# The mixer's output projection as seven half-size products, with the weight sums made in DRAM

## The chip, the cores and the metric

The kernel runs on one core of a Trainium2 chip. The metric is the device time of one execution in microseconds. Three runs of the kernel before took 1121.22, 1121.75 and 1121.85 us. Five engines with queues of their own work side by side: PE (matmul), DVE (elementwise, two inputs), ACT (elementwise, one input, activation functions), POOL, and SP, which here only issues DMAs. PE and DVE and ACT meet through SBUF and through the eight banks of PSUM, each of 128 x 512 floats.

## The reference, cut to what matters

A decoder block on x of shape 1024 tokens x 1024 channels in float32. A mixer makes `merged`, its output projection `mix` goes through a norm into the residual, and an MLP with squared ReLU follows:

```python
merged = (g_pool * jnp.einsum('bsc,cd->bsd', y_pool, w_branch_pool[l])
          + g_attn * jnp.einsum('bsc,cd->bsd', y_attn, w_branch_attn[l]))
mix = jnp.einsum('bsd,de->bse', merged, w_out[l])
x = x + _rmsnorm(mix, g_mix_post[l])
h2 = _rmsnorm(x, g_mlp_pre[l])
ff = jnp.einsum('bsf,fd->bsd', jnp.square(jax.nn.relu(jnp.einsum('bsd,df->bsf', h2, w_up[l]))), w_down[l])
x = x + _rmsnorm(ff, g_mlp_post[l])
```

The change is about the line `mix = ...`, a 1024 x 1024 x 1024 product, and about what it hands to the up projection (`w_up`, 1024 x 4096).

## The kernel before, in words

**Precision.** Each float32 operand is split into a high part (a cast to the reduced type F32R on ACT) and a low part (source minus high, on DVE): `split`, L99 to L104. Every product is made of three passes, high x high, high x low and low x high (`PASSES`, L32). So a 128 x 128 x 512 block costs three matmuls, and every operand costs one ACT and one DVE instruction.

**Stages in order.** Projections for q, k, v and the pooling; attention; the gates; the two branches; the output projection; the up projection; the down projection. The gates, the up and the down projection already run as seven half-size products in place of eight (Winograd's form of Strassen's scheme). The class `Pairs` (L444) does it for gates and up: two output row blocks (a pair p) take two half-size products M1 and M2 (`m1`, `m2`) and then five more (`rest`, L505), whose moving operands are sums of the halves of the activations: B11, B21, B22 as they are and T1 to T4 as sums (`OPERAND`, L442), and whose weights are sums made on DVE in SBUF (`operand`, L458).

**Branches (L897 to L955).** For each of eight channel blocks m a weight block is loaded and split, 24 matmuls of 512 columns run into two PSUM banks, and DVE multiplies with the gate (`branch`, L902). The attention branch makes eight results `za[m]`; then the pool branch makes eight more. `merge` (L928) adds the two halves of the tokens, on POOL for m < 6 and on DVE for m = 6 and 7, and splits the sum: 16 splits of 512 columns.

**Output projection (L963 to L1018 and L1123 to L1138).** Eight blocks of `w_o` are loaded through three staging slots (`stage`, pool `st`) and split (`load_wo`, L940). For each of eight token blocks n, `out_mm` (L986) issues 8 x 3 x 2 = 48 matmuls of 512 columns into two banks. `out_post` (L999) squares the two banks for the norm on ACT, scales them on DVE from PSUM, adds x, stores x1 to DRAM, and scales by the gate's factor into `hs[n]`. Within token block 5 the transposes of the first four token blocks stand (`build_first`, L1044, eight calls, four 128 x 128 transposes each). In `n == 5` up pairs 0 to 2 are prepared.

**Start of the up projection (L1163 to L1201).** M1 and M2 of six pairs (NF0 = 6) run early, as they need only B11 and B21. In their shade `build_second` (L1054) transposes the second four token blocks and makes T2, T1, T3, B22, T4. Then `rest` closes pair after pair.

**What sets the order.** The attention and the first part of the gates are written out by hand. Everything from the `rest` of the gates on is ordered by a planner, which places each instruction when its own estimates say that it can run, in program order among those that are ready; an engine then works through its queue in that order. Buffers are counted: four PSUM banks under the name `mm` and four under `at`, three staging slots `st`, 17 slots `g`, six `wh`, six `ga`, four `y`.

Of the kernel before, what the change touches and what calls it, by code (L numbers as in the profile page):

```python
# [14 lines left out]
P = 128  # L15
# [35 lines left out]
def block_kernel(ctx: ExitStack, tc, xt, x, consts, vecs, sinks, b_qkv, g_post, g_mlp_post,  # L51
                 w_qkv, w_u, w_g, w_pool, w_bp, w_ba, w_o, w_up, w_dn, x1_dram, spill, y_dram, wbp_dram, f_dram, out):
# [391 lines left out]
    class Pairs:  # L444
# [7 lines left out]

        def load(self, f, t=None):
            t = stage([NK, P]) if t is None else t
            nc.sync.dma_start(t, self.src[f])
            self.raw[f] = t

        def operand(self, p, i):  # L458

            r0, r1_ = self.raw[2 * p], self.raw.get(2 * p + 1)  # L460
            if i in (5, 6, 3):
                if p not in self.sums:
                    self.sums[p] = ga_.tile([P, 2, 4, P], F32, tag="ga", name=nm("ws"))
# [371 lines left out]

    def later_builds():
# [60 lines left out]
    def gate_load(m):  # L897
        t = g32([S])
        nc.sync.dma_start(t, z_dram[m])
        return t  # L900

    def branch(w, rhs, z):  # L902
# [3 lines left out]
        for th in range(2):  # L906
            sl = slice(th * 512, (th + 1) * 512)
            dve.tensor_tensor(z[:, sl], z[:, sl], bs[th], ALU.mult)
        return z
# [11 lines left out]
    ysp, za = {}, []  # L921
    for m in range(8):
        za.append(branch(w_ba[m], lambda k, hl, th: asp[th][k // 2][hl][:, k % 2, :], gate_load(8 + m)))
        if m in (2, 3, 5, 6):
            pool_part({2: 1, 3: 0, 5: 2, 6: 3}[m])
    mg = []

    def merge(m, zp):  # L928
        mt = []
        for th in range(2):  # L930
            sl = slice(th * 512, (th + 1) * 512)
            (pool if m < 6 else dve).tensor_tensor(zp[:, sl], zp[:, sl], za[m][:, sl], ALU.add)
            t = ar([2, 512]) if th == 1 and 1 <= m <= 6 else gr([2, 512])
            split(t[:, 0, :], t[:, 1, :], zp[:, sl])
            mt.append(t)
        mg.append(mt)

    wos = []

    def load_wo(k, tile_):  # L940
        s_ = stage([D])
        nc.sync.dma_start(s_, w_o[k])
        hi, lo = tile_("wohi"), tile_("wolo")
        split(hi, lo, s_)
        wos.append((hi, lo))

    def wo_early(name):
        return yy.tile([P, D], F32R, tag="y", name=nm(name))
# [14 lines left out]
    for k in range(2, NK):  # L963
        if k == 3:
            merge(7, zp)
            gpost_b = bcast(g_post, D)
        load_wo(k, lambda name: wo.tile([P, D], F32R, tag="wo", name=nm(name)))
# [16 lines left out]
    obs = {}  # L984

    def out_mm(n, ks):  # L986
        th, i = n // 4, n % 4
        if n not in obs:
            tag = "at" if n in (0,) else "mm"
            obs[n] = bank(tag), bank(tag)  # L990
        for k in ks:
            for hl in range(2):
                l = mg[k][th][:, hl, i * P:(i + 1) * P]
                for whl in range(2 - hl):
                    for dj in range(2):
                        pe.matmul(obs[n][dj], l, wos[k][whl][:, dj * 512:(dj + 1) * 512],  # L996
                                  start=k == 0 and hl == 0 and whl == 0, stop=k == NK - 1 and hl == 1)

    def out_post(n):  # L999

        bs = obs.pop(n)
        xs = stage([D])
        nc.sync.dma_start(xs, x[n])
        t = (bcp.tile([P, D], F32, tag="bc", name=nm("x1")) if n == 4 else
             xq.tile([P, D], F32, tag="x1", name=nm("x1")))
        r = mean_sq(bs, halves(t))
        for dj in range(2):
            sl = slice(dj * 512, (dj + 1) * 512)
            dve.scalar_tensor_tensor(t[:, sl], bs[dj], r, gpost_b[:, sl], ALU.mult, ALU.mult)
# [3 lines left out]
        hs[n] = t  # L1013
# [24 lines left out]
    def tr_block(th, k):  # L1038
        b = bank("at", [4, P])
# [4 lines left out]
    def build_first(kt, h):  # L1044
        if h == 0:
            raw[kt] = g32([2, 512])
        k = 4 * h + kt
        b = tr_block(0, k)
# [5 lines left out]
    def build_second(kt):  # L1054
        b12, b22 = tr_block(1, kt), tr_block(1, 4 + kt)
        if kt % 2:
            tmp = stage([2, 512])
        else:
            tmp = ga_.tile([P, 2, 512], F32, tag="ga", name=nm("tt"))
# [5 lines left out]
        dve.scalar_tensor_tensor(t3, b22, gain(4 + kt), t3, ALU.mult, ALU.subtract)  # L1065
        dve.tensor_tensor(r21, r21, t2, ALU.subtract)
        for name, src in (("T2", t2), ("T1", r11), ("T3", t3), ("B22", b22), ("T4", r21)):
            if name == "B22":
                t = ar([2, 512])
            else:  # L1070
                t = (yy.tile([P, 2, 512], F32R, tag="y", name=nm(name)) if kt == 0 else
                     fp.tile([P, 2, 512], F32R, tag="T", name=nm(name)))
            if name == "B22":
                split_gain(t, src, 4 + kt)
            else:
                split(t[:, 0, :], t[:, 1, :], src)
            X[name][kt] = t

# [38 lines left out]
    def up_big(shape):  # L1117
        return xq.tile([P] + shape, F32R, tag="x1", name=nm("wx"))

    up = Pairs(w_up, up_big, lambda: g32([S]), up_close_first, up_close0, up_close1)  # L1120
    X = up.X

    for ks in (range(NK - 1), range(NK - 1, NK)):  # L1123
        out_mm(0, ks)
        out_mm(1, ks)
    out_post(0)
    out_post(1)
    for n in range(2, NT):
        if n == 5:
            for k in range(NK):  # L1130
                out_mm(n, (k,))
                build_first(k // 2, k % 2)
        else:
            out_mm(n, range(NK))
        out_post(n)
        if n == 5:
            for p in range(3):
                up.prepare(p)  # L1138
# [5 lines left out]
    gfin_b = bcast(g_mlp_post, D)  # L1144
    NP = NF // 2
    NF0 = 6
# [24 lines left out]
    for p in range(3):  # L1171
        up.m1(p, bank("mm"))
    build_second(0)
    up.m2(0)
    up.m1(3, bank("mm"))
    build_second(1)
    up.m2(1)
    up.m1(4, bank("mm"))
    up.prepare(5)
    up.operand(0, 6)  # L1180
    b6, b7 = bank("at"), bank("at")
    build_second(2)
    up.m2(2)
    for i in (7, 5, 4, 3):
        up.operand(0, i)
    up.m2(4)
    up.m1(5, bank("mm"))
    first_kt(0)
    build_second(3)
    up.m2(3)  # L1190
    first_kt(1)
    up.m2(5)
    first_kt(2)
    first_kt(3)
# [5 lines left out]
    up.rest(0, ga_.tile([P, S], F32, tag="ga", name="f1_first"), b6, b7, bank("at"), done=(6, 7),  # L1200
# [28 lines left out]
    flush()  # L1229
    fpool.__exit__(None, None, None)  # L1230
# [233 lines left out]
```

## Time and profile before

| what | value |
|---|---|
| median of 3 runs | 1121.75 us |
| profiled execution | 1121.68 us |
| its span | 1119.9 us (1.78 us lie around it) |
| PE busy | 1110.1 us, 99% |
| DVE busy | 791.9 us, 71% |
| ACT busy | 536.5 us, 48% |
| POOL busy | 62.6 us, 6% |
| granted PE clock | 0.999 |

PE, the matmul engine, is busy nearly throughout, so a term of the sum is an amount of PE work taken away or a gap put into it. The shares of DVE and ACT are means over stages that differ much, and are read by stage below.

### The profile page before, as it was taken

How to read it: one execution, taken by the hardware profiler on the slowest of the kernel's cores; microseconds unless marked ns; L12 is line 12 of the kernel's file. 1: busy time of each engine (PE TensorE's matmuls, PEld its weight loads, DVE VectorE, ACT ScalarE, POOL GpSimd, SP SyncE). 2: the span in 40 equal slices, each digit the busy share in tenths (PEclk: the TensorE clock that was granted, in tenths of full speed). 3: DMA queues.
4: the chain of work that ended last, by engine and by line, in shares of the span. 5: the costliest groups of instructions: out<-in, count | busy, mean ns of one | idle time of the engine just before them, and what ended most of it. 6: DMA issues, size and time to landing. Idle time of an engine off the chain costs nothing.

```text
span 1119.9 us, 13921 instructions
## 1 busy us (share of the span) xinstructions
PE 1110.1 (99%) x5167; PEld 918.8 (82%) x5167; DVE 791.9 (71%) x1158; ACT 536.5 (48%) x904; POOL 62.6 (6%) x105
## 2 busy tenths in 40 slices
PE   9999999999999999999999999999999999999997
PEld 8888788888888888888888888888888888888885
DVE  5478867899768873458988767666547945447797
ACT  7466656444432333547555645354434445344342
POOL 0333210000000410000000000000000000000000
PEclk9999999999999999999999999999999999999999
DMA  9406569356672543323466554535597765332652
GB/s 350 136 11 137 147 154 307 131 188 209 242 251 69 198 144 129 131 99 120 155 221 245 198 209 158 188 122 184 201 366 250 246 198 189 97 99 72 215 194 95
DMA packets 82484, 197.41 MB, mean 176 GB/s; under 512 B 7153, under 2 KB 19569, under 8 KB 82417
## 3 DMA queue, kind: packets, MB, share of 16 engines
q1 hardware_dynamic: 72448, 174.78, 46.4%
q10 hardware_dynamic: 5616, 19.66, 4.6%
q0 software_dynamic: 4352, 2.10, 1.7%
q8 instruction: 40, 0.66, 0.2%
q14 instruction: 28, 0.22, 0.1%
HBM read 140.94 MB, written 55.57 MB: 175 GB/s over the span
## 4 chain that ended last, share of the span: by engine, by line
PE 92%; DVE 5%; ACT 1%; DMA 1%; issue 0%; DVEq 0%; SPq 0%
PE mm L491 23%; PE at L491 16%; PE at L1302 15%; PE mm L1302 12%; PE mm L996 7%; PE mm L428 5%; PE mm L187 3%; PE mm L430 3%; PE mm L581 2%; PE at L196 1%; PE sc L187 1%; PE at L996 1%; PE at L399 1%; PE sc L335 1%; PE mm L196 1%; PE at L1041 1%
## 5 line engine op out<-in xcount | busy, mean ns | idle before, releaser
L1302 PE MATMUL at<-ar,wh 128*128 128x512 f32 x744 | 169.6, 389 | 0.0
L1302 PEld LDWEIGHTS at<-ar,wh 128*128 128x128 f32 x744 | 139.6, 188 | 29.3 <-DVE ar L104 0.4
L1302 PE MATMUL mm<-ar,wh 128*128 128x512 f32 x576 | 131.0, 389 | 0.0
L1302 PEld LDWEIGHTS mm<-ar,wh 128*128 128x128 f32 x576 | 108.1, 188 | 22.5
L104 DVE TENSOR_TENSOR wh<-raw,wh 128x1024 fp32r<-128x1024 f32 x53 | 64.8, 1223 | 83.1 <-ACT wh L101 83.0
L101 ACT CAST wh<-raw 128x1024 fp32r<-128x1024 f32 x53 | 55.8, 1052 | 133.8 <-PE at L1302 60.9
L101 ACT CAST wh<-st 128x512 fp32r<-128x512 f32 (+1 forms) x105 | 66.5, 643 | 76.9 <-PE at L491 20.9
L104 DVE TENSOR_TENSOR wh<-st,wh 128x512 fp32r<-128x512 f32 (+1 forms) x105 | 78.2, 754 | 28.6 <-ACT wh L101 26.1
L491 PE MATMUL mm<-gr,wh 128*128 128x512 f32 x309 | 74.1, 390 | 0.0
L491 PEld LDWEIGHTS mm<-gr,wh 128*128 128x128 f32 x309 | 57.7, 188 | 11.8
L491 PE MATMUL mm<-T,wx 128*128 128x512 f32 x288 | 67.4, 389 | 0.0
L491 PEld LDWEIGHTS mm<-T,wx 128*128 128x128 f32 x288 | 54.1, 188 | 11.2
L491 PE MATMUL at<-T,wx 128*128 128x512 f32 x252 | 59.4, 389 | 0.0
L491 PEld LDWEIGHTS at<-T,wx 128*128 128x128 f32 x252 | 47.3, 188 | 9.8
L491 PE MATMUL mm<-x,wh 128*128 128x512 f32 x240 | 55.2, 389 | 0.0
L491 PEld LDWEIGHTS mm<-x,wh 128*128 128x128 f32 x240 | 45.0, 188 | 9.4
L104 DVE TENSOR_TENSOR ar<-B,ar 128x1024 fp32r<-128x1024 f32 x37 | 45.1, 1219 | 6.3 <-ACT ar L101 6.1
L581 PE MATMUL mm<-x,wh 128*128 128x512 f32 x192 | 47.8, 396 | 0.0
L101 ACT CAST ar<-B 128x1024 fp32r<-128x1024 f32 x37 | 38.9, 1051 | 8.5 <-DMA B<-in_w_dn_dram 5.7
L491 PE MATMUL at<-gr,wh 128*128 128x512 f32 x174 | 42.5, 390 | 0.0
L581 PEld LDWEIGHTS mm<-x,wh 128*128 128x128 f32 x192 | 35.2, 188 | 7.7
L491 PEld LDWEIGHTS at<-gr,wh 128*128 128x128 f32 x174 | 32.6, 188 | 7.2 <-DVE gr L104 0.5
(363 smaller groups left out, 2147.6 us busy)
## 6 DMA issues: line engine op xcount, KB each, us to landing
raw<-f_dram SPq DMA_DIRECT2D x53, 512.0 KB, 3.8
f_dram<-g SPq DMA_DIRECT2D x30, 512.0 KB, 3.4
B<-in_w_dn_dram SPq DMA_DIRECT2D x24, 512.0 KB, 6.0
st<-in_w_up_dram SPq DMA_DIRECT2D x23, 512.0 KB, 3.6
st<-in_w_g_dram SPq DMA_DIRECT2D x18, 512.0 KB, 4.2
f_dram<-g ACTq DMA_DIRECT2D x17, 512.0 KB, 2.6
g<-spill_dram SPq DMA_DIRECT2D x16, 512.0 KB, 4.6
raw<-in_w_dn_dram SPq DMA_DIRECT2D x16, 512.0 KB, 4.6
```

The source lines that it names most:

```text
L101: act.copy(hi, src)
L104: eng.tensor_tensor(lo, src, f32(hi), ALU.subtract)
L187: pe.matmul(bq, xs_[k][n // 4][:, xh, n % 4 * P:(n % 4 + 1) * P], wq[k][:, h, :], start=k == 0 and j == 0, stop=k == NK - 1 and j == 2)
L196: pe.matmul(bkv_of(n), xs_[k][n // 4][:, xh, n % 4 * P:(n % 4 + 1) * P], wkv[k // 2][:, h, k % 2, :], start=k == 0 and j == 0 and not (joi ...
L335: pe.matmul(sb[:, kv, i, :nk], qt[r, qx, m * P:(m + 1) * P], kx[r, k0:k0 + nk], start=j == 0, stop=j == 2)
L399: pe.matmul(flat(yb), v[:, kv, :], flat(p[:, 4 * kv:4 * kv + 4]), start=j == 0, stop=j == len(mms) - 1)
L428: pe.matmul(bs[th], whi[:, k, :], rhs(k, hl, th), start=k == 0 and hl == 0, stop=False)
L430: pe.matmul(bs[th], wlo[:, k, :], rhs(k, 0, th), start=False, stop=k == nk - 1)
L491: pe.matmul(b, w[:, wh, kt, :], xo[kt][:, xh, :], start=not after and kt == 0 and j == 0, stop=kt == 3 and j == 2, skip_group_check=after)
L581: pe.matmul(b, (whi, wlo)[h][:, k, :], xr(k, xh, th), start=j == 0, stop=j == len(mms) - 1)
L996: pe.matmul(obs[n][dj], l, wos[k][whl][:, dj * 512:(dj + 1) * 512], start=k == 0 and hl == 0 and whl == 0, stop=k == NK - 1 and hl == 1)
L1302: pe.matmul(bs[t], fo[fh][:, k2, t * P:(t + 1) * P], wo_[wh][:, k2, :], start=not after and s2 == 0 and k2 == 0 and j == 0, stop=s2 == NS ...
```

## The change

The output projection becomes seven products of half size, as in gates, up and down. The 1024 x 1024 activations `merged` are cut by channel half and token half into b11, b12, b21, b22; `w_o` into four quarters `W_Q`. Product i has a 512 x 512 x 512 block: four token blocks t, four channel blocks kt, three passes, 48 matmuls.

**Weight sums.** Products 5, 6, 7 and 3 need sums of quarters. They are made in DRAM, in a new tensor of four 1 MB parts: a plain DMA copies a quarter and a DMA issued by POOL with `accum_op` adds another. Four copies stand in SP's queue in the gates' loop; eight accumulating and four plain DMAs stand in POOL's queue after it, and parts 6 and 3 build on those before them.

**Merging.** The gated branches are kept as pairs of channel blocks per token half. Three of the four merges are DMAs issued by POOL that add SBUF to SBUF; the last is on DVE. Activation sums are formed in place on DVE, with the sign of half of the columns turned, which `gpost_b` undoes.

**Products.** Order 1, 5, 6, 3, 7, then 2 and 4 in turn by token block. 1, 6, 7, 4 accumulate in the `at` banks, 5 and 3 and then 2 in the `mm` banks, with copies and adds into `hs` between. Four `build_first` calls (the h = 0 ones) stand in the last two products, four in the up stage.

**Up.** Seven pairs begin early (NF0 = 7); `build_second` makes T2, T3 and B22, and the new `build_third` splits T1 and T4 last. Some tiles move to other pools.

```diff
@@ gates loop, and after it
+            if p in (2, 3, 4, 5):
+                sl = TWO[p % 2]
+                nc.sync.dma_start(W_O[5 if p < 4 else 7][sl], W_Q[1, 0][sl])
...
+    for sl in TWO:
+        pool.dma_start(W_O[5][sl], W_Q[1, 1][sl], accum_op=ALU.add)
+    for sl in TWO:
+        pool.dma_start(W_O[7][sl], W_Q[0, 0][sl], accum_op=ALU.add)
+    for dst, term in ((6, W_Q[0, 0]), (3, W_Q[0, 1])):
+        for sl in TWO:
+            pool.dma_start(W_O[dst][sl], W_O[{6: 5, 3: 6}[dst]][sl])
+        for sl in TWO:
+            pool.dma_start(W_O[dst][sl], term[sl], accum_op=ALU.add)
...
+    def merge(j):
+        for z, zp in zip(zg[8, j], zg.pop((0, j))):
+            if j < 3:
+                pool.dma_start(z, zp, accum_op=ALU.add)
+            else:
+                dve.tensor_tensor(z, z, zp, ALU.add)
...
     for m in range(8):
-        if m in (4, 6):
-            load_wo(m // 2 - 2, wo_early)
-        zp = branch(wbp_dram[m], lambda k, hl, th: ysp[k][hl][:, th * 512:(th + 1) * 512], gate_load(m))
-        if m < 7:
-            merge(m, zp)
+        branch(wbp_dram[m], lambda k, hl, th: ysp[k][hl][:, th * 512:(th + 1) * 512], 0, m)
+        if m % 2:
+            merge(m // 2)
+        if m == 0:
+            wo_weight(1, x_place)
+        elif m == 2:
+            wo_weight(5, x_place)
+        elif m == 5:
+            b11, b12 = merged(0, 1), merged(0, 0)
+            gop[1] = split_pairs(b11, gr)
+            for p_, q_ in zip(b11, b12):
+                dve.tensor_tensor(p_, p_, q_, ALU.subtract)
+        elif m == 6:
+            gop[5] = split_pairs(b11, ar)
...
+    def wo_mm(i, bs, after=False, blocks=()):
+        for t in range(4):
+            for kt in range(4):
+                for j, (gh, wh) in enumerate(PASSES):
+                    pe.matmul(bs[t], gop[i][kt // 2][gh][:, kt % 2, t * P:(t + 1) * P], wop[i][kt // 2][wh][:, kt % 2],
+                              start=not after and kt == 0 and j == 0, stop=kt == 3 and j == 2, skip_group_check=after)
+                if (t, kt) in blocks:
+                    build_first(*blocks[t, kt])
+            yield t
...
-    for n in range(2, NT):
-        if n == 5:
-            for k in range(NK):
-                out_mm(n, (k,))
-                build_first(k // 2, k % 2)
-        else:
-            out_mm(n, range(NK))
-        out_post(n)
...
+    for t in wo_mm(1, X4):
+        act.copy(hs[4 + t][:, :512], X4[t])
+    for p_, q_ in zip(b11, b22):
+        dve.scalar_tensor_tensor(p_, p_, -1.0, q_, ALU.mult, ALU.subtract)
+    gop[6] = split_pairs(b11, gr)
+    wo_weight(6, wslot)
...
+    for t in wo_mm(5, Y4):
+        act.copy(hs[t][:, 512:], Y4[t])
+    wo_weight(3, o_place)
+    gop[3] = split_pairs(b22, o_place)
+    for t in wo_mm(6, X4, True):
+        act.copy(hs[t][:, :512], X4[t])
...
+    for t in wo_mm(3, Y4, True):
+        dve.tensor_tensor(hs[t][:, :512], hs[t][:, :512], Y4[t], ALU.add)
+    gop[2] = split_pairs(b21, ar)
+    wo_weight(2, gr)
...
+    for p in range(3):
+        up.prepare(p)
+    for t in wo_mm(7, X4, True):
+        dve.tensor_tensor(hs[t][:, 512:], hs[t][:, 512:], X4[t], ALU.add)
+        out_post(t, hs[t][:, 512:])
+    Y4 = [bank("mm") for _ in range(4)]
+    p2 = wo_mm(2, Y4, False, {(3, 0): (1, 0), (3, 2): (2, 0)})
+    p4 = wo_mm(4, X4, True, {(2, 2): (0, 0), (3, 0): (3, 0)})
+    for t in p2:
+        dve.tensor_tensor(hs[4 + t][:, :512], hs[4 + t][:, :512], Y4[t], ALU.add)
+        next(p4)
+        if t < 3:
+            out_post(4 + t, X4[t])
...
-    NF0 = 6
+    NF0 = 7
...
-    for p in range(3):
+    for p in range(4):
         up.m1(p, bank("mm"))
+        for kt in (range(2 * p, 2 * p + 2) if p < 2 else ()):
+            build_first(kt, 1)
     build_second(0)
     up.m2(0)
...
     first_kt(0)
-    build_second(3)
     up.m2(3)
     first_kt(1)
     up.m2(5)
+    build_third(2)
+    build_third(3)
```

Here `W_O[i]` is the weight of product i (1, 2 and 4 are quarters of `w_o`, 5, 6, 7 and 3 the four new parts), `TWO` the two halves of a quarter, `merged(kh, th)` the two pair tiles of a channel and token half, `split_pairs` two splits of 1024 columns, `wo_weight` two loads and two such splits.

More of the change, by code (lines that the diff above doesn't have):

```diff
@@ L894, in block_kernel, with gate_pair, branch @@
                 b4=None if p else bank("mm"))
[L897 to L902, printed above, removed]
+    zg = {}
+    def gate_pair(base, j):
+        zg[base, j] = [g32([2, 512]) for _ in range(2)]
+        for th, t in enumerate(zg[base, j]):
+            nc.sync.dma_start(t, z_dram[base + 2 * j:base + 2 * j + 2, :, th * 512:(th + 1) * 512]
+                              .rearrange("m p n -> p m n"))
+    def branch(w, rhs, base, m):
+        if m % 2 == 0:
+            gate_pair(base, m // 2)
+        z = zg[base, m // 2]
         whi, wlo = load_w(w, [4, P])
@@ L919, in pool_part @@
         ysp[gi] = hi, lo
-    ysp, za = {}, []
+    ysp = {}
     for m in range(8):
-        za.append(branch(w_ba[m], lambda k, hl, th: asp[th][k // 2][hl][:, k % 2, :], gate_load(8 + m)))
+        branch(w_ba[m], lambda k, hl, th: asp[th][k // 2][hl][:, k % 2, :], 8, m)
         if m in (2, 3, 5, 6):
             pool_part({2: 1, 3: 0, 5: 2, 6: 3}[m])
[L926 to L936, printed above, removed]
@@ new lines, in block_kernel, with split_pairs, wo_weight, merged @@
+    gop, wop = {}, {}
+    def split_pairs(srcs, place):
+        ops = [(place([2, 512]), place([2, 512])) for _ in srcs]
+        for (hi, lo), t in zip(ops, srcs):
+            split(hi, lo, t)
+        return ops
+    def wo_weight(i, place):
+        ts = []
+        for sl in TWO:
+            t = stage([2, 512])
+            nc.sync.dma_start(t, W_O[i][sl].rearrange("k p n -> p k n"))
+            ts.append(t)
+        wop[i] = split_pairs(ts, place)
+    def merged(kh, th):
+        return [zg[8, 2 * kh + j][th] for j in range(2)]
@@ L962, in block_kernel, with o_place, xq_tile, yy_tile @@
     wo = opool.__enter__()
[L963 to L967, printed above, removed]
+    def o_place(shape):
+        return wo.tile([P] + shape, F32R, tag="wo", name=nm("wo"))
+    def xq_tile(shape, dt=F32R, name="x1"):
+        return xq.tile([P] + shape, dt, tag="x1", name=nm(name))
+    def yy_tile(shape, dt=F32R, name="x1"):
+        return yy.tile([P] + shape, dt, tag="y", name=nm(name))
+    gpost_b = bcast(g_post, D)
+    act.activation(gpost_b[:, 512:], gpost_b[:, 512:], AF.Identity, scale=-1.0)
+    junk_o = bcp.tile([P, 1024], F32, tag="bc", name="junk_o")[:, :512]
     def mean_sq(src_halves, junk_halves):
@@ L982, in block_kernel, with out_post @@
     hs = [None] * NT
[L984 to L1001, printed above, removed]
+    def wo_mm(i, bs, after=False, blocks=()):
[7 more added lines that the diff above has]
+            yield t
+    def out_post(n, second):
+        t = hs[n]
+        src = t[:, :512], second
         xs = stage([D])
         nc.sync.dma_start(xs, x[n])
-        t = (bcp.tile([P, D], F32, tag="bc", name=nm("x1")) if n == 4 else
-             xq.tile([P, D], F32, tag="x1", name=nm("x1")))
-        r = mean_sq(bs, halves(t))
+        r = mean_sq(src, (junk_o, junk_o))
         for dj in range(2):
             sl = slice(dj * 512, (dj + 1) * 512)
-            dve.scalar_tensor_tensor(t[:, sl], bs[dj], r, gpost_b[:, sl], ALU.mult, ALU.mult)
+            dve.scalar_tensor_tensor(t[:, sl], src[dj], r, gpost_b[:, sl], ALU.mult, ALU.mult)
         dve.tensor_tensor(xs, xs, t, ALU.add)
@@ L1139, in block_kernel @@
+    Y4 = [bank("mm") for _ in range(4)]
[6 more added lines that the diff above has]
+            out_post(4 + t, X4[t])
+    for t in (3,):
+        out_post(4 + t, X4[t])
     opool.__exit__(None, None, None)
@@ L1179, in block_kernel @@
     up.prepare(5)
+    build_second(1)
     up.operand(0, 6)
-    b6, b7 = bank("at"), bank("at")
[L1182 to L1187, printed above, removed]
+    up.m1(5, bank("mm"))
+    up.m2(2)
+    up.prepare(6)
+    build_second(2)
+    build_third(0)
+    up.operand(0, 7)
+    up.m2(4)
+    up.m1(6, bank("mm"))
+    b6, b7 = bank("at"), bank("at")
+    build_third(1)
+    build_second(3)
     first_kt(0)
-    build_second(3)
     up.m2(3)
@@ L1192, in block_kernel @@
     up.m2(5)
+    build_third(2)
+    build_third(3)
+    for i in (5, 4, 3):
+        up.operand(0, i)
     first_kt(2)
+    up.m2(6)
     first_kt(3)
```

97 lines of the change are left out of this document (49 added, 48 removed).

## The prediction

> **What bounds the kernel now.** I read the page's totals first, then who PE waited for, then the stretch of the output projection in the chain of waits, then the busy time by stage. First the totals and the PE row of the 40 slices, and the list of all waits of PE.
>
> ```profile
> span 1119.9 us, 13921 instructions
> PE 1110.1 (99%) x5167; PEld 918.8 (82%) x5167; DVE 791.9 (71%) x1158; ACT 536.5 (48%) x904; POOL 62.6 (6%) x105
> PE   9999999999999999999999999999999999999997
> ```
> ```profile
> PE mm L205 <- DVE zeros L183: 1.5, 1, 1.5
> PE at L399 <- DVE qt L104: 0.4, 1, 0.4
> PE sc L335 <- DVE s L344: 0.3, 1, 0.3
> PE at L491 <- DVE g L519: 0.2, 1, 0.2
> ```
>
> PE sets the time: four waits, 2.4 us in all, none in the output projection. So matmuls taken away are time taken away, unless the change opens gaps. The price of a matmul comes from the chain of waits (start, duration, what):
>
> ```profile
> 477.05 21.81 PE mm L996 x96
> ...
> 513.39 0.87 PE at L1041 x8
> ...
> 543.30 2.72 PE mm L491 x12
> ```
>
> 21.81 / 96 = 0.227 us for each 512-column matmul, 0.87 / 8 = 0.109 for a transpose; 12 matmuls take 2.72. Next, busy time by stage (window, PE, PEld, DVE, ACT, POOL, clock, DMA share, GB/s): output projection; up until its first T1 and T4 products; the closing of the early pairs; then a stretch of the gates, and one token block of the projection.
>
> ```profile
> 407.60:498.70 91.10, 91.10 (x418) 75.10 (x417) 44.53 (x89) 39.62 (x74) 0.00 (x0) 1.00 0.39 133
> 498.70:540.40 41.70, 41.70 (x201) 34.82 (x200) 36.17 (x61) 28.87 (x54) 0.00 (x0) 1.00 0.35 116
> 540.40:620.00 79.60, 79.38 (x350) 65.20 (x349) 67.22 (x110) 42.77 (x62) 0.00 (x0) 1.00 0.61 217
> ...
> 220.00:300.00 80.00, 80.00 (x355) 66.24 (x354) 73.41 (x111) 39.25 (x52) 0.00 (x0) 1.00 0.63 213
> ```
> ```profile
> 450.00:460.00 10.00, 10.00 (x45) 8.26 (x44) 3.64 (x9) 2.72 (x6) 0.00 (x0) 1.00 0.23 91
> ```
>
> In the projection DVE is busy 44.53 of 91.10 us, half idle. In the up start it is busy 36.17 of 41.70. The change spends DVE time exactly where it is free, and just ahead of where it isn't.
>
> **The change part by part.**
>
> *PE.* Removed: 8 x 48 = 384 matmuls; added 7 x 48 = 336. That is 48 x 0.227 = 10.9 us less. The 32 early transposes stay, 16 of them moved behind the projection; the seventh pair's M1 and M2 are only moved ahead. The stage becomes 336 x 0.227 + 16 x 0.109 = 78.0 us, and the up start 41.7 + 24 x 0.227 + 16 x 0.109 = 48.9.
>
> *DVE and ACT.* Prices by form (line, shapes, count, busy us, mean ns):
>
> ```profile
> L104 DVE TENSOR_TENSOR wolo<-st,wohi 128x1024 fp32r<-128x1024 f32 x6 | 7.2, 1220 | 2.2 <-ACT wohi L101 2.2
> L104 DVE TENSOR_TENSOR wh<-st,wh 128x512 fp32r<-128x512 f32 x6 | 4.0, 686 | 0.3 <-ACT wh L101 0.3
> L1034 DVE SCALAR_TENSOR_TENSOR gr<-at,vec,gr 128x512 fp32r<-128x512 f32 x8 | 5.8, 746 | 3.5 <-ACT gr L1033 3.5
> L908 DVE TENSOR_TENSOR g<-g,mm 128x512 f32<-128x512 f32 x2 | 1.3, 683 | 1.5 <-PE mm L430 1.5
> ...
> L101 ACT CAST wohi<-st 128x1024 fp32r<-128x1024 f32 x8 | 8.3, 1051 | 7.6 <-DMA st<-in_w_o_dram 5.5 <-PE mm L428 2.1
> ...
> L498 ACT COPY g<-mm 128x512 f32<-128x512 f32 x6 | 3.5, 583 | 0.1
> ```
>
> DVE from the start of product 1 to the last token block:
> - the last gate products and the last merge: 2 x 0.68 + 2 x 1.22 = 3.8
> - operands of 6, 7, 4 formed in place, 6 instructions of 1024 columns. The scalar form is not in the trace at that width on SBUF; between 1.22 (plain) and 2 x 0.746, I take 1.45 for the four of 6 and 4, so 4 x 1.45 + 2 x 1.22 = 8.2
> - splits of 1024 columns: two of activations and two of weights in each of products 6, 3, 7, 2, 4 (those of 1 and 5 fall into the branches): 20 x 1.22 = 24.4
> - adds of products 3, 7, 2 out of PSUM: 12 x 0.69 = 8.2
> - three prepared pairs, 6 x 0.69 = 4.1, and four builds, 4 x 0.75 = 3.0
> - eight `out_post`, each as the 450 to 460 row has it, 3.64: 29.1
>
> Sum 80.8 us in a stage of 78.0; it was 44.5 in 91.1. Up start: 36.2 - 3.6 (the last `out_post`, counted above) + 3.0 (four builds moved in) + 1.4 (one more prepared pair) = 37.0 of 48.9. Together 117.8 of 126.9 us, 93%. In the gates' row DVE ran at 73.41 / 80 = 92% and PE lost nothing. So demand stands at what the trace shows DVE can deliver beside a full PE, with 9.1 us to lose in waits. If it idles 8% of 127 us, as in that row, 10 us go and T1 and T4 come 1 to 2 us late; if its queue never runs dry, nothing. I take 1.5 us there, bounds 0 and 6. Inside the projection I charge nothing: operands wait for data of the branches and for slots, not for the product just before. Through product 7's splits DVE has 3.8 + 5.3 + 12 x 1.22 = 24 us of work, and 43.6 us (four products of 10.9) until that product begins; through product 4's, with the first adds, 39 of 54. That room is the cover; without it each late pair of splits costs 1.05 + 1.22 = 2.3 us.
>
> ACT gains 12 copies out of PSUM (12 x 0.58 = 7 us) and wider casts; at 39.62 of 91.10 it has room.
>
> *Staging.* Three slots now pass 10 loads of weights, 3 of up and 8 of x in 78 us. With about 8, 6 and 11 us each (loads 3.6 to 4.2 us, the split, a store of 2.6, estimated from the rows below), 186 of 234 slot-us. Nothing charged.
>
> *POOL's queue, which the trace does not show at this size.* The accumulating DMAs and their one relative (q1 and q0: packets, MB, share of 16 engines; then issues; then issue time on POOL; then the present merges on POOL, whose bracket is idle time):
>
> ```profile
> q1 hardware_dynamic: 72448, 174.78, 46.4%
> ...
> q0 software_dynamic: 4352, 2.10, 1.7%
> ```
> ```profile
> st<-in_w_o_dram SPq DMA_DIRECT2D x8, 512.0 KB, 3.6
> st<-in_x_dram SPq DMA_DIRECT2D x8, 512.0 KB, 4.1
> x_dram<-st SPq DMA_DIRECT2D x8, 512.0 KB, 2.6
> ...
> y_dram<-yt POOLq DMA_DIRECT2D x16, 128.0 KB, 4.5
> ```
> ```profile
> L404 POOL DMA_DIRECT2D y_dram<-yt x16: 1004/1016/1181, 82.8 to 178.8; - x16
> ```
> ```profile
> 203.22 0.42 SPq L455 DMA_DIRECT2D g<-in_w_g_dram  x1
> ```
> ```profile
> 370.28 2.98 POOL L932 TENSOR_TENSOR g<-g,g 128x512 f32<-128x512 f32 x2 [190.51 <-DVE g L908]
> ...
> 386.73 2.99 POOL L932 TENSOR_TENSOR g<-g,g 128x512 f32<-128x512 f32 x2 [2.05 <-DVE g L908]
> ```
>
> q1 moved 174.78 MB in 46.4% of 1119.9 us: 336 GB/s, 21 per engine. q0 moved 2.10 MB in 1.7%: 110 GB/s, 6.9 per engine. An accumulation of 0.52 MB lies between 3.6 us (a plain load) and 18 (four times the 4.5 us of 128 KB); I take 8, the 4.5 plus 0.39 MB more at q0's 110 GB/s. Twelve DMAs on POOL, one after the other at the worst: 96 us, from about 205 (SP is then in the gates' loop, the 203.22 row) to 300; at 18 us each, to 420. POOL is idle for 190 us up to 370, nothing stands behind them but the merges, and part 3, the last made, is read near 425. Taken as hidden. Their issue costs POOL 12 x 1.0 us. The four copies on SP add 4 x 0.4 us of issue to a queue that waits for slots there.
>
> [...]
>
> *Merges.* The one that product 1 hangs on is that of blocks 2 and 3, ready at 386.7; two DMAs of 8 us, even in a row, land by 403, and the split behind the second (1.05 + 1.22) ends at 405; product 1 begins at 407.6. Taken: nothing. At 18 us each in a row it is 17 us late; a gain isn't possible, as PE has no gap there.
>
> Sum, against the profiled 1121.68 (span 1119.9, 1.78 around it; 0.07 from the median): 1121.7 - 10.9 + 1.5 = **1112.3 us**.
>
> **The rivals.**
>
> *DVE overruns.* For it: 117.8 of 126.9 us, and the next stage stands at 67.22 of 79.60 already, so lateness is handed on and not caught up. Against: PE may take M1 and M2 of other pairs first. If DVE idles 15 to 20% of the 127 us, it loses 19 to 25, so 10 to 16 beyond its room; if PE finds other pairs' M1 and M2 for half of that, 5 to 8 us stay: 1116 to 1119. At 20 us beyond the room the gain is gone: 1120 to 1124.
>
> [...]
>
> *Merges late.* From 9 us a DMA on product 1 waits, and at 13 the gain is spent (2 x 13 + 2.3 after 386.7 is 415, 7.4 us late, with the 1.5 above); at 18, 1112.3 + 17 = 1129. Against: the two may run side by side.
>
> *The matmuls do not get away*: if the new pattern of operands cost the PE more per matmul, 336 x 0.26 would equal the old stage: 1122. Against: L491 with the same pattern shows 0.227.
>
> **How the numbers follow.** Forecast case (1110.8 to 1114.5): 0.60. DVE overrun with part of the gain left (1114.5 to 1119.5): 0.21; with the gain gone (1119.5 to 1125): 0.07. Sums late: 0.06, slower. Merges late: 0.05, of which 0.02 by a few us and still faster. Matmuls dearer: 0.01. Faster by over 0.2% means below 1119.5, which is about what a measurement of this kernel can tell: 0.60 + 0.21 + 0.02 = 0.83. Within 0.2%: 0.06. Slower: 0.11. The range runs from 1110.0, just below the sum without any stall (1110.8), to 1120.5; about 0.15 lies above it.
>
> **What would show it.** Right: PE records at 0.227 us in the new line of the products, seven groups of 48, no idle in front of them; DVE above 9 tenths from 407 to 540; the T products starting near 535, with an idle of 0 to 4 us whose releaser is DVE's split of T1 or T4; POOL's DMA landings near 8 us and the last of the sums before 330. Wrong: idle in front of products 6, 3 or 7 released by a DMA into `st` (sums), in front of product 1 released by a DMA into `g` (merges), or idle in front of the up products above 5 us (DVE). If PE's busy time falls by 10.9 us and the span by less, the difference is in those waits.

## The result and the profile after

Nine runs of the changed kernel took 1114.22 to 1119.59 us, median **1115.63**, beside nine of the kernel before with a median of 1121.85: a ratio of 0.9948 (95% interval 0.9933 to 0.9963). That is 6.2 us faster; the forecast was 9.4. The profiled execution took 1114.22 us, 7.5 less than the profiled one of before; it is the fastest of the nine, so its stages show the change at its best. First the totals of the changed kernel's page, then the list of all waits of PE:

```profile
span 1112.4 us, 13921 instructions
PE 1099.5 (99%) x5119; PEld 908.9 (82%) x5119; DVE 807.9 (73%) x1180; ACT 552.4 (50%) x921; POOL 59.8 (5%) x111
```
```profile
PE at L1081 <- DVE x L1050: 1.6, 1, 1.6
PE mm L205 <- DVE zeros L183: 1.5, 1, 1.5
PE mm L428 <- DVE g L933: 1.0, 1, 1.0
...
```

PE's busy time fell by 10.6 us (1110.1 to 1099.5), and two waits are new: 1.0 us in front of a branch product (L428) and 1.6 us in front of transposes in the up start (L1081). Busy time by stage, before and after, each stage cut at the same PE instruction (columns as in the prediction): gates, branches, projection, up start as far as the first product of a `wx` weight, rest of up.

```profile
167.86:320.53 152.67, 152.63 (x674) 125.98 (x672) 125.46 (x188) 72.22 (x106) 2.02 (x2) 1.00 0.64 217
320.53:407.57 87.04, 87.04 (x386) 72.07 (x384) 71.28 (x99) 27.79 (x39) 17.46 (x12) 1.00 0.46 154
407.57:498.69 91.12, 91.12 (x417) 75.13 (x416) 44.56 (x89) 39.63 (x74) 0.00 (x0) 1.00 0.39 133
498.69:548.58 49.89, 49.89 (x238) 41.58 (x236) 44.30 (x74) 33.26 (x61) 0.00 (x0) 1.00 0.32 106
548.58:807.59 259.01, 258.79 (x1141) 213.77 (x1140) 183.78 (x289) 129.14 (x191) 0.00 (x0) 1.00 0.54 194
```
```profile
167.60:320.94 153.34, 153.21 (x674) 125.81 (x672) 124.87 (x188) 72.63 (x107) 11.28 (x14) 1.00 0.88 271
320.94:409.29 88.35, 87.37 (x385) 71.92 (x384) 61.59 (x90) 27.02 (x32) 5.39 (x6) 1.00 0.67 195
409.29:487.35 78.06, 78.06 (x353) 64.66 (x352) 66.83 (x113) 49.53 (x86) 0.00 (x0) 1.00 0.50 166
487.35:546.32 58.97, 57.38 (x278) 47.75 (x277) 53.56 (x89) 42.03 (x76) 0.00 (x0) 1.00 0.38 126
546.32:799.43 253.11, 253.11 (x1118) 209.39 (x1116) 178.67 (x282) 126.86 (x186) 0.00 (x0) 1.00 0.55 199
```

The projection gives 13.06 us, the up start takes 9.08 back, the rest of up gives 5.90: together 9.88 us of gain. Then 1.31 us are lost in the branches and 0.67 in the gates, two stages that lie ahead of the products. What lies ahead of the gates is 0.26 us shorter, and what lies behind up 0.66 us longer. In the gates the share of the DMA engines went from 0.64 to 0.88.

**The branches.** DVE's and ACT's queues there, in order of time (start, duration, instruction, bracket: idle time before it and what ended it):

```profile
400.45 1.23 DVE L104 TENSOR_TENSOR gr<-g,gr 128x1024 fp32r<-128x1024 f32 x1 [6.93 <-ACT gr L101]
401.71 1.22 DVE L992 TENSOR_TENSOR g<-g,g 128x1024 f32<-128x1024 f32 x1
402.85 1.28 DVE L933 TENSOR_TENSOR g<-g,mm 128x512 f32<-128x512 f32 x2
...
399.37 1.05 ACT L101 CAST gr<-g 128x1024 fp32r<-128x1024 f32 x1 [7.30 <-DMA g<-g]
```

The merge of blocks 2 and 3 is a transfer that lands at 399.37. DVE's split of its result stands ahead of the gate product of a later block (L933, 402.85) in DVE's queue. So the gate product comes some 5 us late, its PSUM bank comes free late, and PE waits 0.98 us.

### The profile page after: what moved, and what is told of

It reads as the page before. It is cut to its first block, busy times and chain, and to the rows that moved or that the text cites. A ratio compares the mean times of both kernels' runs of the same rounds, so it can differ in the third digit from the quotient of the medians.

```text
span 1112.4 us, 13921 instructions
## 1 busy us (share of the span) xinstructions
PE 1099.5 (99%) x5119; PEld 908.9 (82%) x5119; DVE 807.9 (73%) x1180; ACT 552.4 (50%) x921; POOL 59.8 (5%) x111
## 4 chain that ended last, share of the span: by engine, by line
PE 82%; DVE 8%; DMA 5%; ACT 2%; issue 2%; DVEq 0%; POOL 0%; POOLq 0%; ACTq 0%; SPq 0%
PE mm L494 24%; PE at L494 16%; PE at L1384 15%; PE mm L1384 12%; PE mm L187 3%; PE mm L584 2%; PE at L1035 2%; DMA g<-g 1%; PE at L196 1%; PE mm L1035 1%; PE sc L187 1%; PE mm L428 1%; PE at L399 1%; DMA g<-spill_dram 1%; DVE gr L104 1%
## 5 line engine op out<-in xcount | busy, mean ns | idle before, releaser
L1384 PE MATMUL at<-ar,wh 128*128 128x512 f32 x744 | 169.6, 389 | 0.0
L494 PE MATMUL mm<-gr,wh 128*128 128x512 f32 x333 | 80.2, 391 | 0.0
L494 PEld LDWEIGHTS mm<-gr,wh 128*128 128x128 f32 x333 | 62.1, 188 | 12.8
L494 PE MATMUL at<-gr,wh 128*128 128x512 f32 x150 | 36.6, 390 | 0.0
L101 ACT CAST wx<-ws 128x512 fp32r<-128x512 f32 x30 | 18.6, 620 | 33.9 <-DVE ws L470 19.1
```

The source lines that it names most:

```text
L101: act.copy(hi, src)
L494: pe.matmul(b, w[:, wh, kt, :], xo[kt][:, xh, :], start=not after and kt == 0 and j == 0, stop=kt == 3 and j == 2, skip_group_check=after)
L1384: pe.matmul(bs[t], fo[fh][:, k2, t * P:(t + 1) * P], wo_[wh][:, k2, :], start=not after and s2 == 0 and k2 == 0 and j == 0, stop=s2 == NS ...
```

## Experiments

The list gives the stages of each profiled execution, cut as above, and the medians of all runs; "sums" are the sixteen transfers that make the weight sums; the execution with the sums early was not cut into stages. Each ratio is against runs of the kernel before on the same chip.

| kernel | gates | branches | projection | up start | median us (lowest to highest, runs) | ratio (95%) |
|---|---|---|---|---|---|---|
| changed, again | 159.10 | 88.55 | 78.06 | 58.40 | 1117.48 (1114.65 to 1124.33, 12) | 0.9969 (0.9954 to 0.9984) |
| DVE merges | 152.77 | 87.04 | 78.06 | 58.50 | 1111.42 (1110.71 to 1113.62, 4) | 0.9912 (0.9900 to 0.9925) |
| DVE merges, again | 154.36 | 87.04 | 78.06 | 58.33 | 1112.84 (1112.35 to 1117.01, 6) | 0.9930 (0.9918 to 0.9941) |
| splits behind gate products | 153.40 | 87.04 | 78.06 | 59.26 | 1117.76 (1113.37 to 1120.10, 7) | 0.9958 (0.9942 to 0.9975) |
| up loads elsewhere | 154.43 | 88.29 | 78.06 | 58.72 | 1116.27 (1114.21 to 1119.75, 6) | 0.9955 (0.9942 to 0.9968) |
| no sums | 152.67 | 88.33 | 78.06 | 58.84 | 1112.15 (1111.88 to 1112.88, 4) | 0.9917 (0.9904 to 0.9930) |
| DVE merges, no sums | 152.69 | 87.04 | 78.06 | 58.49 | 1111.47 (1110.80 to 1112.12, 4) | 0.9910 (0.9897 to 0.9923) |
| DVE merges, T1 and T4 not last | 152.95 | 87.04 | 78.06 | 57.81 | 1112.37 (1110.78 to 1116.17, 6) | 0.9923 (0.9909 to 0.9937) |
| DVE merges, 7.3 us more DVE | 154.63 | 87.04 | 78.06 | 60.92 | 1114.87 (1112.90 to 1116.19, 5) | 0.9940 (0.9928 to 0.9952) |
| DVE merges, sums early | | | | | 1135.27 (1130.65 to 1140.06, 6) | 1.0127 (1.0105 to 1.0149) |
| DVE merges, sums late | 154.20 | 99.13 | 79.33 | 58.95 | 1137.08 (1133.74 to 1140.30, 5) | 1.0137 (1.0121 to 1.0153) |
| the same, layout kept | 152.76 | 99.89 | 78.06 | 58.67 | 1122.64 (1121.68 to 1124.43, 11) | 1.0012 (1.0003 to 1.0021) |

**The changed kernel once more.**

> The changed kernel once more, as the measure for the three beside it. Queue theory: its 1.0 us wait of PE in the branches (at the gate product of L933) and its 1.6 us wait at the transposes of L1081 come from waits at the head of DVE's and ACT's queues, for a merging transfer and for a staged load of w_up. So both recur: 0.5 to 6 us and 1 to 2 us, the first with the landing time of the second merge, and the median is again 1114 to 1117. Rival (VectorE is overrun): a wait at the T products near 540 us, and none of the other two need recur.

Both waits came back (1.1 and 1.1 us), and a third, larger one with them. The profile is that of an execution of 1120.26 us; the list of PE's waits, the chain of waits (start, duration, what), and two windows of it, the gates and a stretch inside them:

```profile
PE mm L494 <- DVE z L522: 3.3, 1, 3.3
```
```profile
233.64 8.78 DMA st<-in_w_g_dram
...
245.07 8.54 DMA g<-in_w_g_dram
...
253.62 0.69 DVE ws L467
...
263.37 0.69 DVE z L522
...
264.10 4.21 PE mm L494 x9
```
```profile
167.80:326.90 159.10, 155.80 (x673) 127.94 (x672) 125.20 (x188) 72.80 (x107) 11.28 (x14) 0.98 0.85 261
240.00:270.00 30.00, 26.73 (x106) 21.50 (x106) 22.75 (x37) 11.35 (x17) 3.75 (x5) 0.89 0.92 270
```

Two loads of `w_g` take 8.8 and 8.5 us, one behind the other, DVE falls behind, and PE waits 3.3 us. The granted clock is 0.89 in the 30 us around it. So the stage is 6.4 us longer than the 152.67 of before: 3.3 of waiting, 3.2 of dearer matmuls (155.80 us busy against 152.63, the granted clock of the stage 0.98 against 1.00). The runs of the changed kernel differ by up to 10 us, those of the kernel before by less than 2 beside them.

**The merges on DVE again.**

```diff
-            if j < 3:
-                pool.dma_start(z, zp, accum_op=ALU.add)
-            else:
-                dve.tensor_tensor(z, z, zp, ALU.add)
+            dve.tensor_tensor(z, z, zp, ALU.add)
```

> All four merges are DVE additions, as in the kernel before; no accumulating transfer in the tiles. Queue theory: the wait of PE at the gate product of L933 is gone, the branches take 87.0 to 87.6 us (88.35 with the transfers), the stretch of runs is narrower, and the median falls by 0.7 to 2 us against the changed kernel beside it. Rival (VectorE's load decides): six additions of 1.22 us, 7.3 us more on DVE in the branches and the projection, make new waits of PE; the median is 1 to 7 us higher.

```profile
320.00:407.04 87.04, 87.04 (x385) 72.07 (x384) 74.08 (x102) 29.48 (x34) 0.00 (x0) 1.00 0.52 173
```

The branches are back at exactly 87.04 us, without a wait of PE, though DVE has 12.5 us more work there (61.59 to 74.08). DVE's load was not the limit; the wait for the transfer was. The median fell by 6.1 us against the changed kernel beside it, three times what was expected; the branches account for 1.3 to 1.5 of it.

**The transfers kept, only their place in the queue mended.** `gop[1]`'s second split, the subtractions and `gop[5]`'s splits are queued behind the gate products of blocks 5 and 6:

```diff
-            gop[1] = split_pairs(b11, gr)
-            for p_, q_ in zip(b11, b12):
-                dve.tensor_tensor(p_, p_, q_, ALU.subtract)
+            gop[1] = split_pairs(b11[:1], gr)
+            with tc.issue_after(done.ins):
+                gop[1] += split_pairs(b11[1:], gr)
+                for p_, q_ in zip(b11, b12):
+                    dve.tensor_tensor(p_, p_, q_, ALU.subtract)
```

> The merges stay transfers, but DVE's splits and subtractions that wait for the second merge stand behind the gate products of blocks 5 and 6 in DVE's queue, not ahead of them. Queue theory: the gate product of block 5 comes at 396 to 398 us, not 402.85, PE's wait before block 7 is gone, the branches take 87.0 to 87.6 us; the first product of the projection could start up to 1 us late if the splits come too late. Median 0.5 to 2 us below the changed kernel beside it. Rival (the price is in the transfer itself, its traffic or its time): the branches stay at 88 us or more.

```profile
321.11:408.15 87.04, 87.04 (x385) 72.07 (x384) 63.79 (x93) 27.62 (x33) 5.38 (x6) 1.00 0.71 208
```
```profile
397.25 1.28 DVE L933 TENSOR_TENSOR g<-g,mm 128x512 f32<-128x512 f32 x2 [3.55 <-PE mm L430]
398.45 1.22 DVE L104 TENSOR_TENSOR gr<-g,gr 128x1024 fp32r<-128x1024 f32 x1
```

The gate product comes at 397.25, and the branches take 87.04 us at a DMA share of 0.71, more than the changed kernel's 0.67. So those 1.3 us were the place of the waiting instruction in DVE's queue, not the transfer's traffic. The median did not fall as expected: three of the seven runs, at 1113.37 to 1113.56, lie below all 21 of the changed kernel, four at 1117.76 and above. The spread from the gates covers the gain.

**The up loads out of the staging slots** (`up.prepare(p, g32([NK, P]))` in place of `up.prepare(p)` for pairs 0 to 3).

> The w_up loads of pairs 0 to 3 go into the free 4 KB buffers instead of the three staging slots that the x loads use too. Queue theory: the wait of 1.6 us before the transposes of L1081 is gone and the up start (from the end of the last product to the T4 product's end) is 57.2 to 57.8 us instead of 58.97; median 1.0 to 1.8 us below the changed kernel beside it. Rival (DVE has no room there): a wait of about the same size appears at another place of the stage, and the median is within 0.5 us.

The chain of waits of the changed kernel had given the idea (start, duration, what):

```profile
489.25 3.66 DMA st<-in_w_up_dram
...
495.11 0.76 DVE x L1050
```

A load that had waited for a slot, and behind its split, in DVE's queue, the last `out_post`, whose bank the transposes need. With other buffers that wait is gone, but others stand further on:

```profile
PE at L494 <- DVE wh L104: 0.5, 1, 0.5
PE at L494 <- DVE ar L1074: 0.4, 1, 0.4
```

The up start is 58.72 us against 58.97, not the 57.2 to 57.8 expected. The rival holds for the stage: the slot only decided where DVE's lateness showed. The median lies 1.2 us below the changed kernel beside it, but with runs from 1114.21 to 1119.75 that tells nothing about this stage.

**No sums.** The sixteen transfers go, and `W_O` names plain quarters for products 5, 6, 7 and 3.

> The sixteen transfers that make the four weight sums are left out, and products 5, 6, 7 and 3 read plain quarters of w_o in their place, so that the output projection's result is not the reference's; all else as in the changed kernel, merges by transfer too. Traffic theory: these transfers slow the gates' own loads (one of w_g took 8.8 us, and PE waited 3.3 us in the gates of one execution), so without them the gates take 152.5 to 152.9 us in every execution, the runs lie within 4 us instead of within 10, and the median falls by 2 to 5 us against the changed kernel (1115.6 to 1117.5). Rival (the spread comes from the merges by transfer alone): runs up to 1120 remain, and the median falls by less than 1 us.

Issues with median times to landing: the gates' loads first in the changed kernel, with the sums' transfers, then without them.

```profile
st<-in_w_g_dram SPq DMA_DIRECT2D x18, 512.0 KB, 6.9
ws_dram<-in_w_o_dram POOLq DMA_DIRECT2D x8, 512.0 KB, 8.5
g<-g POOLq DMA_DIRECT2D x6, 512.0 KB, 6.4
ws_dram<-in_w_o_dram SPq DMA_DIRECT2D x4, 512.0 KB, 7.8
ws_dram<-ws_dram POOLq DMA_DIRECT2D x4, 512.0 KB, 6.9
```
```profile
st<-in_w_g_dram SPq DMA_DIRECT2D x18, 512.0 KB, 4.2
```

A gate load takes 4.2 us without the sums, as before the change, and 6.9 with them. The gates are back at 152.67 us, the four runs lie within 1.0 us, and the median is 1112.15: the traffic theory holds, and its rival, that the spread came from the merges, falls. SP's own four copies are not what held up the two slow loads: in that execution they were issued by 199 us, and POOL's last seven transfers between 229 and 262, beside the loads of 233.64 and 245.07. The 1.3 us in the branches stay (88.33), as they must.

**Neither sums nor merges by transfer.**

> All merges on DVE and the sixteen transfers of the weight sums left out; products 5, 6, 7 and 3 read plain quarters of w_o, so that the output projection's result is not the reference's. It is the floor: what the change is worth where neither its merges nor its sums cost anything. If the two costs are separate and add up: gates 152.5 to 152.9, branches 87.04, median 1109.8 to 1111.2, runs within 2 us. If one is only the other's consequence: as the changed kernel without sums, 1111.9 to 1112.9.

1111.47 us: the floor, 0.8 below the forecast. The stages are those of the first theory, the median lies between the two ranges. Taking away either cost alone already gives 1111.4 to 1112.8 where both together cost 4 to 6 us of the medians, so they don't simply add up; the next run bears on that.

**DVE merges once more.**

> All merges on DVE once more, sums in the gates as in the changed kernel: whether its narrow runs (1110.7 to 1113.6 in four) were chance. Traffic theory: with the sums' transfers still in the gates, runs above 1114 turn up, and the median lies 1 to 3 us above that of the kernel without sums. Rival (the spread came from the merges by transfer): all within 1110.5 to 1113.7.

1112.84, with runs of 1114.41 and 1117.01, and 0.8 us of waiting in the gates: the sums' cost is there, as the traffic theory has it, 1.4 us above the floor. Up to the end of the gates the queues of this kernel are those of the changed one: PE, DVE, ACT and POOL run the same instructions in the same order in both traces. Why its large waits there seem rarer (2 of its 10 runs lie over 3 us above the fastest, against 9 of 21) stays open; at these numbers it can be chance, beside the 1.3 us that it saves for certain.

**T1 and T4 not last** (DVE merges; `build_third(kt)` stands at the end of `build_second(kt)`).

> All merges on DVE, and T1 and T4 are split beside T2 and T3, not last. If DVE's queue decides in the up start, as the sum on record has it, the products that need T2 and T3 come later behind these eight splits of 0.68 us: a new wait of PE of 1 to 5 us in the up start, median 1112 to 1117 (1111.4 with the merges on DVE alone). If DVE has the room: the up start stays at 58.5 us, median 1110.7 to 1112.

The up start is 57.81 us against 58.50, and no wait at the T products. DVE had the room; the late place of T1 and T4 is worth nothing here. (The median of 1112.37 is 0.4 above the range for that case; its runs reach up to 1116.17.)

**7.3 us more DVE** (DVE merges; six subtractions of 1.22 us for products 7, 2 and 4 are done twice).

> All merges on DVE, and six of DVE's subtractions of 1.22 us in the projection (the low parts of the operands of products 7, 2 and 4) are done twice, 7.3 us more of DVE, with the same result. If DVE has 9 us of room up to T1 and T4 (the sum on record), the transposes' wait stays near 1.1 us and the time rises by 0 to 1.5 us. Rival (DVE is overrun, its queue is full from 440 us on): the extra work comes back as 4 to 7 us of PE's waits, at the transposes of L1078 and in the up start; median 1115 to 1119.

```profile
PE mm L494 <- ACT g L1119: 1.1, 1, 1.1
PE at L494 <- DVE z L522: 1.0, 2, 0.7
PE at L494 <- DVE ar L1073: 0.6, 1, 0.6
```

The projection did not feel it (78.06); the up start grew by 2.4 us, half in small waits (2.37 us idle against 1.13), half in dearer matmuls around them (58.55 us busy against 57.37). Neither theory had the size. If the room is what did not come back, 7.3 - 2.4, DVE had an estimated 5 us left. The larger rise of the median, 2.0 to 3.5 us, includes the gates (154.63, with 0.7 us of the waits for L522).

**The sums early, at 30 to 165 us.**

> All merges on DVE, and the sixteen transfers of the weight sums moved from the gates to the first 130 us, where the DMA engines are 5 to 60 per cent busy. Traffic theory: gates 152.5 to 152.9 us, branches 87.0, projection 78.06, runs within 2 us, median 1109.5 to 1111.5. Rival (the transfers cost wherever they lie): the first stage (167.2 to 167.8 us now) gets 1 to 4 us longer, because POOL's queue, which carries attention's small operations, waits for them; the median is then 1112 to 1115.

In this edit the copy for product 5 stands behind its addition, so part 5, and 6 and 3 that build on it, lack a quarter; the transfers are as many. The rival was right in kind, and far too small: +23 us against the DVE merges alone.

```profile
PE mm L522 <- ACT wh L101: 9.8, 1, 9.8
PE sc L361 <- DVE s L370: 5.7, 2, 5.3
```

15.5 us of new waits in these two, in attention and in the first gates. POOL's queue also carries attention's small operations, and before the additions issued at 76.66, 85.75 and 95.61 us it stood idle for 5.3, 6.3 and 9.0 us. How much of it is POOL's and how much SP's queue was not told apart.

**The sums late.** Only the sum for product 5 is made in the gates; the other twelve transfers start behind a POOL copy of 8 columns out of the first branch's result, into a new tile of 32 bytes a partition.

> All merges on DVE; in the gates only the sum for product 5 is made (four transfers), the other twelve transfers start when the first branch product is through, at about 325 us, on POOL's queue, which has nothing else by then. They form a chain of six links of 6 to 9 us, so the last sum is ready at 360 to 380 us, and its weights are loaded after 410. Traffic theory: gates 152.5 to 152.9 us in every execution, branches 87.0 to 87.5 us, runs within 3 us, median 1109.8 to 1111.3. Rival (the branches' loads are as tight as the gates'): new waits of PE in the branches of 1 to 4 us, median 1112 to 1115.

The rival again, but at 25 us. The branches took 99.13 us, with 7.6 of PE's waits. But 12 us more lay behind the up start, where nothing differs (cut at the same instruction, 3.6 in the rest of up and 8.7 in the down stage). The groups of matmuls (columns: names out<-in, shapes, count, busy us, mean ns) show what was dearer there:

```profile
L1386 PE MATMUL at<-ar,wh 128*128 128x512 f32 x744 | 174.4, 395 | 0.0
...
L494 PE MATMUL mm<-gr,wh 128*128 128x512 f32 x333 | 82.2, 396 | 0.0
L494 PE MATMUL mm<-T,wx 128*128 128x512 f32 x288 | 68.0, 390 | 0.0
...
L494 PE MATMUL mm<-gr,ar 128*128 128x512 f32 x108 | 26.5, 390 | 0.0
...
L1037 PE MATMUL mm<-wo,ar 128*128 128x512 f32 x48 | 11.4, 396 | 0.0
...
L1037 PE MATMUL mm<-wo,wo 128*128 128x512 f32 x48 | 11.1, 389 | 0.0
```

The first name is the moving operand of 512 columns, the second the stationary one. The traces hold no addresses; what was moved follows from the order and the side of the pools in the kernel. `ar` and `gr` lie in pools that are laid out behind the pool with the new tile, so 32 bytes further on than before; `T` and `wo` lie in pools laid out from the other end, and the weights `wh` and `wx` were not moved either. Dear are the groups here of which one operand was moved and the other not, the moving one (`ar,wh`, `gr,wh`, 395 and 396 ns) or the stationary one (`wo,ar`, 396). Where both were moved (`gr,ar`, 390), or neither (`T,wx`, `wo,wo`, 390 and 389), the price lies within 1 ns of the 389 that these groups have in the changed kernel or with the DVE merges.

**The same with the layout kept:** the copy goes into the existing buffer `rb`.

> The kernel with the late sums again, but the small tile that POOL's first copy writes takes an existing buffer in place of 32 bytes of its own, so that every later pool of SBUF lies where it lay before. In that kernel's profile a matmul of the down stage starts every 0.233 us against 0.227, at a granted clock that reads 1.00, and 12 of its 27 us more lie there, far behind the sums. Layout theory (operands that start 32 bytes further make matmuls dearer): every stage is back at 0.227, the down stage at 312.5 us, the gates at 152.5 to 152.9, the waits of the branches stay (5 to 10 us with the lower clock behind them), median 1117 to 1124. Rival (the waits or the traffic bring the slower matmuls): they stay at 0.230 to 0.233, median 1133 to 1140 again.

```profile
L1386 PE MATMUL at<-ar,wh 128*128 128x512 f32 x744 | 169.6, 389 | 0.0
...
L494 PE MATMUL mm<-gr,wh 128*128 128x512 f32 x333 | 80.1, 391 | 0.0
...
L1037 PE MATMUL mm<-wo,ar 128*128 128x512 f32 x48 | 11.0, 389 | 0.0
```
```profile
320.39:420.28 99.89, 91.03 (x385) 73.91 (x384) 74.29 (x102) 29.08 (x34) 8.81 (x13) 0.97 0.72 214
```

All these groups are back at their old prices, and the median falls by 14.4 us to 1122.64. What is left is the sums' own price in the branches: 12.9 us, of which 8.9 are waits of PE and 4.0 dearer matmuls, some 3 of them by the granted clock (0.03 of 99.9 us). So twelve of the transfers cost more in the branches than all sixteen in the gates, and the whole gain is spent.

## Why the prediction was right, and where it was not

The median of 1115.63 lies inside the range, but not in the forecast case (1110.8 to 1114.5). It lies where the prediction had put an overrun of DVE (1114.5 to 1119.5, chance 0.21), and it got there by two costs that the prediction had put at nothing. So PE's gain was foreseen; that the range held the rest is luck.

**PE** was right: seven groups of 48 without a gap, 78.06 us for the stage, forecast 78.0. From the changed kernel's timeline, the second product, then the first pair's products of T1 and T4 (the first of these two rows begins with six matmuls of T2 and T3):

```profile
420.17 11.04 PE L1035 MATMUL mm<-wo,ar 128*128 128x512 f32 x48
...
536.80 4.24 PE L494 MATMUL at<-T,wh 128*128 128x512 f32 x18
540.88 2.88 PE L494 MATMUL mm<-T,wh 128*128 128x512 f32 x12
```

**DVE** was right in size by luck and wrong in place. The up start grew by 9.08 us, forecast 8.7 (7.2 of work and 1.5 of stall). The 1.5 us stood at T1 and T4; the last of their splits ended at 533.9, some 4 us before T1's product begins. The 1.6 us came at the transposes instead, where the last `out_post` stood behind a weight's split. The demand was put too high:

```profile
409.29:536.19 126.90, 125.31 (x585) 104.03 (x584) 110.30 (x184) 85.86 (x151) 0.00 (x0) 1.00 0.45 149
```

110.3 us of 126.9, not 117.8, so 87% and not the 9 tenths that were to be seen. Part of the surplus came from adding mean durations: neighbouring DVE records overlap, and the 113 of the projection last 74.2 us in sum where the busy time is 66.83. Yet PE lost 1.6 us, as room on the mean is not room at each instruction. From the load run, an estimated 5 us were left, not 9.1. "Inside the projection I charge nothing" held, with 7.3 us more work too.

**Staging**, "Nothing charged": the slots did delay a load, and taking them out of the way gained 0.25 us of that stage. Right in the sum.

**Merges**, "Taken: nothing", is the first step that failed. The transfers were sized well (6.4 us at the median against 8, and the second of the pair landed at 399.37, before the 403 of the sum). But the sum asked only when product 1 needs them. It did not ask what stands behind the waiting split in DVE's queue: the gate products. Price: 1.3 us.

**Weight sums**, "Taken as hidden", is the second and the larger. The additions took 8.5 us against 8; the last was issued at 254 us and landed 8.2 us later, long before 330. So the dependences were covered. Late sums (chance 0.06) did not come: the copies took 7.8 us from SP's queue and 6.9 from POOL's, the additions 8.5, less than half of the 18 us each at which the chain was put to end at 420. Over how many DMA engines one such transfer is spread, no run here shows. But I had called the sums hidden because nobody waited for them, and left out whom they share the DMA engines with: the gates' loads went from 4.2 to 6.9 us. That cost 0.7 us in the profiled execution, 6.4 in another, and 3.5 to 5.3 of the medians (1115.63 and 1117.48 against 1112.15). The row of the gates in the prediction had a DMA share of 0.63 in it, and I read only DVE from it.

Where neither step costs anything the time is 1111.47, against 1112.3. None of the rivals came true as written: DVE's lateness, the sums and the merges each cost something, in a place that I had not looked at.

The best kernel measured that computes the whole is the changed one with its merges on DVE: 1111.42 and 1112.84 us.

## What to carry to other kernels

- A transfer that nobody waits for can still have a price, in the loads beside it: with the sums' transfers the gates' loads took 6.9 us, without them 4.2. Read the DMA share of the stage it runs in, and which of that stage's loads have an engine waiting for them. Moving it to a quieter stage can be worse: here all sixteen cost 0.7 to 6.4 us in the gates and some 23 in attention and the first gates, and twelve of them 13 in the branches.
- When an addition on an engine becomes a transfer, look at the first instruction that waits for its landing, and at what is queued behind that one; the arithmetic it saves may be worth less. Here six additions became transfers, and the branches took 1.3 us more.
- A test that adds a small buffer may move others: here 32 bytes a partition came with 14.4 us. Keep the layout, or show that the untouched stages kept their prices.

## What the hardware showed that I had not expected

- **The price of a matmul changed with where its operands lie.** Two kernels that differ in one line, the sums late and the same with the layout kept, show it. With one operand of a matmul of 512 columns 32 bytes further on and the other where it was, its record took 395 or 396 ns against 389 to 391, 744 of them 174.4 us against 169.6, at a granted clock that read 1.00 in both; over the whole kernel 14.4 us (medians of 1137.08 and 1122.64). It was the same with the moving operand moved (`ar,wh`, 395) and with the stationary one (`wo,ar`, 396), and with both moved (`gr,ar`) the price was 390. In attention twelve products `wkv,x` of 256 columns, also with one operand moved, took 1.56 us against 1.59 or 1.60. So in these groups it is not the address of one operand alone; which distances are dear, and why, was not tried.
- **The long waits of PE cost more than themselves here.** 3.3 us of waiting in the gates made the stage 6.4 us longer, at a granted clock of 0.89 in the 30 us around it; 8.9 us in the branches made it 12.9, at 0.97. The short ones cost little more: 0.98 us made 1.31, and with 1.6 us in the up start PE was busy for 57.38 us there, against 57.40 in the run with a wait of 0.4.
